# Making the rotary tables earlier and packing attention weights on another engine, in a two-layer encoder kernel

## The chip, the core and the metric

The kernel runs on one core of a Trainium2 chip. A core has five engines that run their own instruction streams in order and wait for one another through semaphores: PE (TensorE, matrix multiply), DVE (VectorE), ACT (ScalarE), POOL (GpSimd) and SP, which here only issues transfers from device memory. The metric is device time in microseconds (us); the lower the better. What one queue issues in a row is carried by 16 transfer engines.

## What is computed

Two layers of a streaming encoder over 256 positions of width 1024. The change lies in the first mixer, multi-head latent attention. Cut to that:

```python
mod = silu(c) @ ada_w[i] + ada_b[i]
sh1, sc1, g1, sh2, sc2, g2 = jnp.split(mod, 6, axis=-1)
h = modulate(rmsnorm(x, norm_g[i, 0]), sh1, sc1)        # h * (1 + sc1) + sh1
proj = h @ w_in                                         # 1024 -> 384 + 256 + 32
c_q  = rmsnorm(proj[..., :384], q_norm)
c_kv = rmsnorm(proj[..., 384:640], kv_norm)
ang = positions[..., None] * inv_freq                   # rotary tables
cos, sin = jnp.cos(ang), jnp.sin(ang)
k_rope = apply_rope(proj[..., 640:], cos, sin)
q  = (c_q @ w_uq).reshape(..., 16, 64 + 32)             # per head: 64 plain, 32 rotary columns
kv = (c_kv @ w_ukv).reshape(..., 16, 64 + 64)           # per head: 64 of the key, 64 of the value
q_rope = apply_rope(q[..., 64:], cos, sin)
o = softmax over the chunk-causal mask of (q_nope k_nope + q_rope k_rope) * scale, times v
x = x + g1 * (o @ w_out)
```

A dense feed-forward layer, a Mamba-2 mixer and a mixture of eight experts follow; the change does not touch them.

## The kernel before

Everything is 128 partitions wide. Activations are held transposed (`xT`, `h32`: 8 chunks of 128 features by 256 positions). Weights come in 1 MB pieces into eight buffers called `raw`; a new piece can only be issued once the instructions that read an old one have let its buffer go. The order in which instructions stand on each engine is not the order of the program text: a scheduler of the framework sets it when the kernel is built, from its own estimate of when each thing is ready, and from then on each engine runs its list strictly in order.

The start, in the order of the text: SP issues the first half of the constants (`cst`), x, small vectors (`vecs`), the modulation weights of units 0 and 2, two pieces of `w_in`, units 1 and 3, the last piece of `w_in`, the positions (`pos_i`, 128 KB, L407) and the rest of the constants. ACT squares x and takes a root (L413, L415), DVE makes the reciprocal `r` of it (L416), PE transposes x (L421) and spreads `r` over the partitions (L317). The modulation rows of a unit are eight matmuls (L247), a copy by DVE (`row`, L250) and four tiny matmuls (L258); then come the gains (L261, L269), the modulated activations (`tt` L330 on DVE, `h` L332 on ACT) and the projection with `w_in` (L438), first with chunks 0 to 3, and after units 1 and 3 with chunks 4 to 7.

The rotary tables (`ct`, `st`, L447 to L466) are made after that: DVE turns the positions into angles and brings them into range with eleven short instructions of 256 columns, each of which needs the one before it, and ACT takes two sines, ahead of which it loads the table of that function. They are first read by the rotation of the key (L499, L500).

GpSimd fills the mask rows of `qT` and `kT` (L471 to L478) with eight memsets that it begins at once, and copies the rotated key to the other heads (L521).

[...] A block of heads (L596) is its queries, two pairs of heads of attention (scores L570 and L571, maxima L573 and L574, exponentials L577 and L579, scaling L582 and L583, transposes L586 and their copy `pT` L588, values L591 to L593, `aT` L159), and a modulation unit whose sum DVE makes in seven long steps (`acc`, L220, 512 columns each).

Of the kernel before, what the change touches and what calls it, by code (L numbers as in the profile page):

```python
# [20 lines left out]
P = 128  # L21
S = 256
# [47 lines left out]
def rows(ap, n, off=0):  # L70

    return bass.AP(tensor=ap.tensor, offset=ap.offset + off, ap=[[P, n], [1, P]])


def bcast(ap, n, off=0, parts=P):

    return bass.AP(tensor=ap.tensor, offset=ap.offset + off, ap=[[0, parts], [1, n]])
# [3 lines left out]
def body(ctx: ExitStack, tc, x, c, positions, ada_w, ada_b, norm_g,  # L81
# [69 lines left out]
    def packed(src):  # L151

        k, h, n = src.shape[1:]
        t = hlp.tile([P, 1024], F32, tag="whi", name="wcp")[:, :k * h * n]
        A.copy(t.rearrange("p (k h n) -> p k h n", k=k, h=h), src)
        return t.rearrange("p (k m) -> p k m", k=k)

    def split(hi, lo, src):
# [94 lines left out]
    def ada_columns(units, rows):  # L253

        ps = pt("m")
        for i, (u, row) in enumerate(zip(units, rows)):
            for m in range(4):
                PE.matmul(ps[:, 4 * i + m:4 * i + m + 1], row[:, m * P:(m + 1) * P], one4, start=i == m == 0,  # L258
                          stop=True, skip_group_check=True)
        for i, u in enumerate(units):  # L260
            V.tensor_add(mod[:, 0, 4 * u:4 * u + 4], ps[:, 4 * i:4 * i + 4], vecT[:, 0, 4 * u:4 * u + 4])  # L261
# [3 lines left out]
    def make_gsc(i, t, k0=0, k1=DC):  # L265

        sc = mod[:, i, 24 * t + 8 + k0:24 * t + 8 + k1]
        g = vecT[:, 0, 96 + 16 * i + 8 * t + k0:96 + 16 * i + 8 * t + k1]
        V.scalar_tensor_tensor(gsc[:, i, t, k0:k1], sc, 1.0, g, op0=ALU.add, op1=ALU.mult)  # L269
# [108 lines left out]
    with ExitStack() as lctx:  # L378
# [11 lines left out]
        SP.dma_start(cst[:, 0:C_V], consts[:, 0:C_V])  # L390
        x_in = load(x[0], 2)
        V.reduce_sum(one4, ident.rearrange("p (g q) -> p g q", g=4)[:, :, 0], axis=AX.X)
        SP.dma_start(vecs[0:96, 0, :], rows(ada_b, 96))
        SP.dma_start(vecs[96:128, 0, :], rows(norm_g, 32))
        aw = {0: ada_load(0, 0)}
# [7 lines left out]
        u3 = ada_w[0, :, 1536:2048]  # L403
        aw[3] = [load(u3[0:512, :], 4), load(u3[512:768, :], 2), load(u3[768:1024, :], 2)]
        win += [win_load(6, 2)]
        pos_i = mi.tile([P, S], I32, tag="t2", name="pos_i", bufs=2)
        SP.dma_start(pos_i, bcast(positions, S))  # L407
        SP.dma_start(cst[:, C_V:], consts[:, C_V:C_KEY])


# [6 lines left out]
        for q in range(4):  # L417
            ps = pt("mm")
            for i in range(4):
# [2 lines left out]
            A.copy(xT[:, 2 * q:2 * q + 2, :], ps.rearrange("p (a s) -> p a s", a=2))  # L422
        r = spread(pt("n"), r)
        vec_block(0, 128)
        ada_columns((0, 2), [ada_rows(aw[u]) for u in (0, 2)])
        make_gsc(0, 0, 0, 4)
        normmod(0, 0, r, range(4), whole=h32)

        ps_kv, ps_rq, ps_q = pt("mm"), pt("mm"), pt("mm")

        kv = [(ps_kv[:, t * S:(t + 1) * S], t == 0, slice(QL + t * P, QL + (t + 1) * P)) for t in range(2)]
        rq = [(ps_rq[:, 0:S], True, slice(2 * P, 3 * P)),
              (ps_rq[:ROPE, S:2 * S], False, slice(QL + KVL, QL + KVL + ROPE))]
        qq = [(ps_q[:, t * S:(t + 1) * S], t == 0, slice(t * P, (t + 1) * P)) for t in range(2)]

        def win_mm(k, regions):
            for ps, first, sl in regions:
                PE.matmul(ps, win[k // 3][:, k % 3, sl], h32[:, k, :], start=first and k == 0, stop=k == DC - 1,  # L438
                          skip_group_check=True)
        for k in range(4):  # L440
            win_mm(k, kv + rq + qq)
        ada_columns((1, 3), [ada_rows(aw[u]) for u in (1, 3)])
        make_gsc(0, 0, 4, 8)
        normmod(0, 0, r, range(4, 8), whole=h32)


        ct = mp.tile([P, S], F32, name="ct")  # L447
        st = mp.tile([P, S], F32, name="st")
# [15 lines left out]
        A.activation(st, ang, AF.Sin)  # L464
        V.scalar_tensor_tensor(kk, ang, -1.0, ang, op0=ALU.mult, op1=ALU.max)
        A.activation(ct, kk, AF.Sin, bias=halfpi, scale=-1.0)  # L466


        qT = mp.tile([98, NH, S], F32, name="qT")
# [1132 lines left out]
```

## Time and profile before

| | us |
|---|---|
| median of 3 runs | 1297.62 |
| lowest and highest of them | 1292.73, 1299.51 |
| the profiled execution | 1294.19 |
| its span, from first to last instruction | 1292.4 |
| PE busy in the span | 1243.5 |
| DVE, ACT, POOL busy | 841.1, 695.4, 16.9 |

The rows of the profile are times in one execution. "Busy" of PE is modelled and includes waits of a started matmul, so what bounds a stretch is better read from the chain of waits, which goes back from the last instruction to what released it. A timeline row gives the start, the length, the engine, the source line, the operation, what it writes and reads, and how many instructions are merged; in brackets is how long the engine had been idle and what ended it. An fp32 matmul is recorded as two instructions.

### The profile page before, as it was taken

How to read it: one execution, taken by the hardware profiler on the slowest of the kernel's cores; microseconds unless marked ns; L12 is line 12 of the kernel's file. 1: busy time of each engine (PE TensorE's matmuls, PEld its weight loads, DVE VectorE, ACT ScalarE, POOL GpSimd, SP SyncE). 2: the span in 40 equal slices, each digit the busy share in tenths (PEclk: the TensorE clock that was granted, in tenths of full speed). 3: DMA queues.
4: the chain of work that ended last, by engine and by line, in shares of the span. 5: the costliest groups of instructions: out<-in, count | busy, mean ns of one | idle time of the engine just before them, and what ended most of it. 6: DMA issues, size and time to landing. Idle time of an engine off the chain costs nothing.

```text
span 1292.4 us, 21070 instructions
## 1 busy us (share of the span) xinstructions
PE 1243.5 (96%) x8200; PEld 997.4 (77%) x8200; DVE 841.1 (65%) x1293; ACT 695.4 (54%) x1158; POOL 16.9 (1%) x16
## 2 busy tenths in 40 slices
PE   6999999999999999998999999999999999999996
PEld 4677899999988999996648875488855788888652
DVE  3387787787779788853048870388902789988412
ACT  2468554455567767524157650477603676777302
POOL 4000000000000000000000000000000000000000
PEclk9899989999989999997999999999999999999998
DMA  9786569887933466425999999999999999998895
GB/s 341 284 299 216 196 226 361 317 303 268 339 116 131 148 207 233 164 98 196 422 421 420 420 395 413 420 421 420 384 388 421 421 420 383 391 346 315 327 421 214
DMA packets 104747, 407.96 MB, mean 316 GB/s; under 512 B 10418, under 2 KB 16063, under 8 KB 70975
## 3 DMA queue, kind: packets, MB, share of 16 engines
q1 hardware_dynamic: 104638, 406.53, 81.5%
q8 instruction: 66, 1.08, 0.3%
q14 instruction: 43, 0.34, 0.1%
HBM read 405.46 MB, written 1.05 MB: 315 GB/s over the span
## 4 chain that ended last, share of the span: by engine, by line
PE 88%; DMA 4%; ACT 3%; DVE 3%; issue 1%; SPq 0%; DVEq 0%; ACTq 0%
PE a L1280 18%; PE a L1372 11%; PE y L1325 10%; PE y L1391 4%; PE y L347 3%; PE y L349 3%; PE y L348 3%; PE gu L347 3%; PE gu L349 3%; PE gu L348 3%; PE in L349 2%; PE in L347 2%; PE in L348 2%; DMA raw<-in_moe_w_down_dram 2%; PE mm L438 2%; PE mm L505 2%
## 5 line engine op out<-in xcount | busy, mean ns | idle before, releaser
L159 DVE TENSOR_TENSOR wlo<-raw,whi 128x1024 fp32r<-128x1024 f32 x395 | 466.5, 1219 | 85.9 <-ACT whi L159 84.4
L159 ACT CAST whi<-raw 128x1024 fp32r<-128x1024 f32 x395 | 403.9, 1051 | 188.5 <-PE a L1280 42.5
L1372 PE MATMUL a<-raw,xe 128*64 128x384 f32 (+3 forms) x1280 | 161.5, 412 | 0.0
L1280 PE MATMUL a<-wlo,xe_hi 128*128 128x512 f32 (+1 forms) x464 | 153.6, 344 | 0.3
L1280 PE MATMUL a<-whi,xe_lo 128*128 128x512 f32 (+1 forms) x464 | 152.5, 341 | 0.0
L1372 PEld LDWEIGHTS a<-raw,xe 128*64 128x64 f32 x1280 | 91.8, 135 | 68.1 <-issue 50.9
L1293 DVE TENSOR_TENSOR sg<-sg,a 128x512 f32<-128x512 f32 (+2 forms) x36 | 22.0, 641 | 156.8 <-PE a L1372 144.9
L1280 PE MATMUL a<-whi,xe_hi 128*128 128x256 f32 (+1 forms) x464 | 111.6, 345 | 7.7 <-ACT whi L159 7.7
L220 DVE SCALAR_TENSOR_TENSOR acc<-raw,cond,acc 128x512 f32<-128x512 f32 x140 | 104.3, 757 | 2.8 <-ACT acc L218 1.2
L347 PE MATMUL gu<-hT_hi,whi 128*128 128x256 f32 x352 | 99.9, 284 | 1.2 <-ACT hT_hi L334 1.2
L1280 PEld LDWEIGHTS a<-wlo,xe_hi 128*128 128x128 f32 x464 | 87.5, 189 | 16.4 <-DVE wlo L159 3.6
L348 PE MATMUL gu<-hT_lo,whi 128*128 128x256 f32 x352 | 99.7, 283 | 0.0
L349 PE MATMUL gu<-hT_hi,wlo 128*128 128x256 f32 x352 | 99.4, 282 | 0.0
L1280 PEld LDWEIGHTS a<-whi,xe_lo 128*128 128x128 f32 x464 | 87.6, 189 | 9.8
L1280 PEld LDWEIGHTS a<-whi,xe_hi 128*128 128x128 f32 x464 | 76.1, 188 | 23.9 <-ACT whi L159 14.9
L1391 PE MATMUL y<-raw,at 128*64 128x512 f32 (+1 forms) x364 | 81.4, 586 | 0.9 <-DMA raw<-in_moe_w_down_dram 0.7
L347 PE MATMUL in<-hT_hi,whi 128*128 128x256 f32 (+1 forms) x264 | 76.0, 288 | 0.7 <-DVE r L303 0.7
L349 PE MATMUL in<-hT_hi,wlo 128*128 128x256 f32 (+1 forms) x264 | 75.5, 287 | 0.5 <-DVE wlo L159 0.5
L348 PE MATMUL in<-hT_lo,whi 128*128 128x256 f32 (+1 forms) x264 | 74.7, 283 | 0.0
L347 PEld LDWEIGHTS gu<-hT_hi,whi 128*128 128x128 f32 x352 | 67.3, 191 | 1.4 <-ACT hT_hi L334 1.4
L349 PEld LDWEIGHTS gu<-hT_hi,wlo 128*128 128x128 f32 x352 | 67.4, 192 | 0.0
L348 PEld LDWEIGHTS gu<-hT_lo,whi 128*128 128x128 f32 x352 | 67.3, 191 | 0.0
(398 smaller groups left out, 2245.4 us busy)
## 6 DMA issues: line engine op xcount, KB each, us to landing
raw<-in_moe_w_gate_dram SPq DMA_DIRECT2D x88, 1024.0 KB, 6.7
raw<-in_moe_w_up_dram SPq DMA_DIRECT2D x88, 1024.0 KB, 12.2
raw<-in_moe_w_down_dram SPq DMA_DIRECT2D x85, 1024.0 KB, 15.6
raw<-in_ada_w_dram SPq DMA_DIRECT2D x46, 1024.0 KB, 7.1
raw<-in_ssm_w_in_dram SPq DMA_DIRECT2D x20, 1024.0 KB, 5.3
raw<-in_ffn_w_down_dram SPq DMA_DIRECT2D x11, 1024.0 KB, 8.6
raw<-in_ffn_w_gate_dram SPq DMA_DIRECT2D x10, 1024.0 KB, 8.2
raw<-in_ffn_w_up_dram SPq DMA_DIRECT2D x10, 1024.0 KB, 8.9
```

Source lines behind the costliest of these rows:

```text
L159: return A.copy(hi, src), V.tensor_sub(lo, src, hi)
L220: V.scalar_tensor_tensor(acc, w[k // 4][:, k % 4, :], cond[:, k:k + 1], acc, op0=ALU.mult, op1=ALU.add)
L347: PE.matmul(ps, whi, ahi, start=(first and i == 0), stop=False, skip_group_check=skip)
L348: PE.matmul(ps, whi, alo, start=False, stop=False, skip_group_check=skip)
L349: PE.matmul(ps, wlo, ahi, start=False, stop=(last and i == n - 1), skip_group_check=skip)
L438: PE.matmul(ps, win[k // 3][:, k % 3, sl], h32[:, k, :], start=first and k == 0, stop=k == DC - 1, skip_group_check=True)
L505: PE.matmul(ps, lhs(k), rhs(k), start=(k == 0), stop=(k == n - 1))
L1280: PE.matmul(bank[:, o:o + n], a[:, j, :], w[:, m], start=f, stop=l, skip_group_check=True)
L1293: V.tensor_mul(self.sg[:, sl], self.sg[:, sl], self.acc["u", b][:, :n])
L1325: PE.matmul(self.y[b], a, w[:, b * 512:(b + 1) * 512], start=f, stop=l, skip_group_check=True)
L1372: PE.matmul(bank[FEW * h:FEW * (h + 1), o // 2:(o + n) // 2], self.xhi[:, j, :], w[:, h, :], start=first, stop=last, skip_group_check=True)
L1391: res = PE.matmul(self.y[c0 // 512][FEW * h:FEW * (h + 1), c0 % 512:c0 % 512 + n], self.at[t][:, FEW * h:FEW * (h + 1)], ws[h], start=t == ...
```

## The change

Three edits. The load of the positions is issued right after that of x, ahead of the small vectors and all modulation weights. The block that makes `ct` and `st` is moved, unchanged, ahead of the first modulation columns. And the copies of `packed` are written for GpSimd in place of ACT. Lines from L390 on move with it: the angle block is now L424 to L445, the projection L460.

```diff
@@ packed
         t = hlp.tile([P, 1024], F32, tag="whi", name="wcp")[:, :k * h * n]
-        A.copy(t.rearrange("p (k h n) -> p k h n", k=k, h=h), src)
+        G.tensor_copy(t.rearrange("p (k h n) -> p k h n", k=k, h=h), src)
@@ loads
         x_in = load(x[0], 2)
         V.reduce_sum(one4, ident.rearrange("p (g q) -> p g q", g=4)[:, :, 0], axis=AX.X)
+        pos_i = mi.tile([P, S], I32, tag="t2", name="pos_i", bufs=2)
+        SP.dma_start(pos_i, bcast(positions, S))
         SP.dma_start(vecs[0:96, 0, :], rows(ada_b, 96))
...
         win += [win_load(6, 2)]
-        pos_i = mi.tile([P, S], I32, tag="t2", name="pos_i", bufs=2)
-        SP.dma_start(pos_i, bcast(positions, S))
         SP.dma_start(cst[:, C_V:], consts[:, C_V:C_KEY])
@@ tables: this block now stands behind vec_block(0, 128), ahead of ada_columns((0, 2), ...)
         ct = mp.tile([P, S], F32, name="ct")
         st = mp.tile([P, S], F32, name="st")
         ang = mi.tile([P, S], F32, tag="t1", name="ang", bufs=2)
         kk = mi.tile([P, S], F32, tag="tr", name="kk", bufs=2)
         V.tensor_copy(ang, pos_i)
         V.tensor_scalar(ang, ang, cst[:, C_FREQ:C_FREQ + 1], None, op0=ALU.mult)
         V.tensor_scalar(kk, ang, 1.0 / (2 * math.pi), None, op0=ALU.mult)
         V.tensor_scalar(kk, kk, MAGIC, None, op0=ALU.add)
         V.tensor_scalar(kk, kk, MAGIC, None, op0=ALU.subtract)
...
         for v in pieces:
             V.scalar_tensor_tensor(ang, kk, -v, ang, op0=ALU.mult, op1=ALU.add)
         V.tensor_scalar(ang, ang, 3.1415925, -3.1415925, op0=ALU.min, op1=ALU.max)
         A.activation(st, ang, AF.Sin)
         V.scalar_tensor_tensor(kk, ang, -1.0, ang, op0=ALU.mult, op1=ALU.max)
         A.activation(ct, kk, AF.Sin, bias=halfpi, scale=-1.0)
```

Since a scheduler sets the order, what the edits move is read from the built programs. On DVE, at the start of the program (`one4` is L392, the casts L710 belong to a later layer and were put there as filling), the lines with a plus are new at this place:

```order
 L392 TENSOR_REDUCE few<-cst 128x1
 L710 CAST ej<-cst 128x128 x2
+L430 CAST ang<-pos_i 128x256
+L431 TENSOR_SCALAR ang<-ang,cst 128x256
+L432 TENSOR_SCALAR kk<-ang 128x256
+L433 TENSOR_SCALAR kk<-kk 128x256
+L434 TENSOR_SCALAR kk<-kk 128x256
+L441 SCALAR_TENSOR_TENSOR ang<-kk,ang 128x256 x4
+L442 TENSOR_SCALAR ang<-ang 128x256
+L444 SCALAR_TENSOR_TENSOR kk<-ang 128x256
 L416 RECIPROCAL r<-r 128x2
 L211 COPY vecT<-n 128x128
```

The whole block of angles, eleven instructions, now stands ahead of the reciprocal `r`, which every modulated activation needs; before, it stood among and behind the last `tt` of the second half.

On PE, in the same place (transposes of x, spreading of `r`, and the first two units' modulation rows):

```order
 L421 MATMUL mm<-cst,raw 128x128 x16
-L247 MATMUL mm<-raw,cond 32x512
 L317 MATMUL n<-cst,r 128x128 x2
 L210 MATMUL n<-cst,vecs 128x128
-L247 MATMUL mm<-raw,cond 32x512 x7
+L247 MATMUL mm<-raw,cond 32x512 x8
 L258 MATMUL m<-few,row 128x1 x4
 L247 MATMUL mm<-raw,cond 32x512 x8
```

Before, one of the eight row matmuls of unit 0 stood ahead of the spreading of `r`; now all eight stand behind it.

On ACT, in the attention, around the rotary queries of the second block of heads (`t_662`), before:

```order
L556 ACTIVATE qT<-mm 64x256 x2
L155 COPY wcp<-raw 128x384
L562 ACTIVATE qT<-t_662 32x256 x3
L588 COPY pT<-tp 128x384 x2
L562 ACTIVATE qT<-t_662 32x256
L556 ACTIVATE qT<-mm 64x256 x2
```

and the same place now:

```order
L556 ACTIVATE qT<-mm 64x256
L159 CAST aT_hi<-o 128x256
L556 ACTIVATE qT<-mm 64x256
L562 ACTIVATE qT<-t_662 32x256
L588 COPY pT<-tp 128x384
L562 ACTIVATE qT<-t_662 32x256 x3
L556 ACTIVATE qT<-mm 64x256 x2
L588 COPY pT<-tp 128x384
```

The copy of 384 columns is gone from ACT, and the two `pT`, which stood together, now stand apart, one ahead of three rotary query copies and one behind two plain ones. GpSimd gets ten copies: four (the key's two and the first block's two) ahead of its four copies L521, and six behind them.

## Rows read from the trace of the kernel before

**Rows 1.** The page, chain of waits: shares of the span by engine
```profile
PE 88%; DMA 4%; ACT 3%; DVE 3%; issue 1%; SPq 0%; DVEq 0%; ACTq 0%
```
**Rows 2.** Windows: busy us (x instructions) of PE, PEld, DVE, ACT, POOL; granted clock, DMA, GB/s
```profile
44.00:63.00 19.00, 18.35 (x78) 13.39 (x79) 7.57 (x23) 12.09 (x25) 0.24 (x1) 0.84 0.60 207
80.00:100.00 20.00, 17.84 (x110) 14.56 (x108) 15.38 (x42) 16.98 (x47) 0.00 (x0) 1.00 0.86 307
```
**Rows 3.** Chain of waits at the start: start us, us, engine, tile, line
```profile
11.48 1.43 PE mm L247 x2
12.92 0.64 PE n L317 x4
13.67 1.88 PE mm L247 x14
...
17.37 2.38 PE mm L247 x16
...
23.15 13.25 PE mm L438 x48
```
**Rows 4.** Timeline: the weight load of unit 2's fifth row matmul
```profile
18.67 0.14 PEld L247 LDWEIGHTS mm<-raw,cond 128*32 128x32 f32 x4 [0.37 <-DMA raw<-in_ada_w_dram]
```
**Rows 5.** Timeline of the start, POOL and DVE; the last row for comparison
```profile
0.76 3.51 POOL L471 MEMSET qT<- 2x4096 f32 x1 [0.29 <-POOLq L1590]
...
1.05 3.29 DVE L712 CAST uones<-ones 128x128 fp32r<-128x128 f32 x1
...
4.66 3.57 DVE L710 CAST ej<-cst 128x128 fp32r<-128x128 f32 x2
...
8.02 1.10 POOL L472 MEMSET qT<- 2x1024 f32 x1
...
12.02 0.17 DVE L416 RECIPROCAL r<-r 128x2 f32<-128x2 f32 x1 [3.79 <-ACT r L415]
...
12.62 0.95 POOL L477 MEMSET kT<- 1x1024 f32 x1
...
45.69 0.22 DVE L711 CAST uones<-cst 128x128 fp32r<-128x128 f32 x1
```
**Rows 6.** Timeline: four of the DVE rows that make the angles
```profile
44.37 0.28 DVE L451 CAST ang<-pos_i 128x256 f32<-128x256 int32 x1
...
45.83 0.29 DVE L453 TENSOR_SCALAR kk<-ang 128x256 f32<-128x256 f32 x1
...
46.81 1.80 DVE L462 SCALAR_TENSOR_TENSOR ang<-kk,ang 128x256 f32<-128x256 f32 x4
...
48.97 0.43 DVE L465 SCALAR_TENSOR_TENSOR kk<-ang 128x256 f32<-128x256 f32 x1
```
**Rows 7.** Chain of waits from the second projection half to the queries
```profile
44.65 10.74 PE mm L438 x36
...
64.18 16.36 PE mm L505 x60
```
**Rows 8.** The packing copies: count, ns min/median/max, first and last start, forms
```profile
L155 ACT COPY wcp<-raw x10: 500/816/1047, 51.5 to 96.4; 128x768 f32<-128x768 f32 x4, 128x384 f32<-128x384 f32 x4, 128x1024 f32<-128x1024 f32 x2
```
**Rows 9.** Groups of instructions by shape, POOL: busy us, mean ns, idle before
```profile
L521 POOL COPY kT<-kT 32x1024 f32<-32x1024 f32 x1 | 1.0, 1034 | 0.1
```
**Rows 10.** Timeline: POOL's last copy of the key, and a sum on DVE
```profile
64.97 1.89 POOL L521 COPY kT<-kT 32x2048 f32<-32x2048 f32 x1
...
65.39 2.01 DVE L220 SCALAR_TENSOR_TENSOR acc<-raw,cond,acc 128x512 f32<-128x512 f32 x1
```
**Rows 11.** That sum's line from 60 to 140 us: ns min/median/max, first and last start
```profile
L220 DVE SCALAR_TENSOR_TENSOR acc<-raw,cond,acc x39: 731/747/2010, 65.4 to 137.6; 128x512 f32<-128x512 f32 x39
```
**Rows 12.** Chain of waits in the attention: two ACT steps of it
```profile
96.46 0.40 ACT wcp L155
...
98.19 0.49 ACT pT L588
```
**Rows 13.** SP's own waits from 60 to 120 us: total, times, longest
```profile
SPq L127 <- ACT wcp L155: 14.2, 3, 10.3
```

More of the change, by code (lines that the diff above doesn't have):

```diff
@@ L424, in body @@
         vec_block(0, 128)
[L425 to L444, printed above, removed]
         ct = mp.tile([P, S], F32, name="ct")
@@ L466, in body, with win_mm @@
         A.activation(ct, kk, AF.Sin, bias=halfpi, scale=-1.0)
+        ada_columns((0, 2), [ada_rows(aw[u]) for u in (0, 2)])
+        make_gsc(0, 0, 0, 4)
+        normmod(0, 0, r, range(4), whole=h32)
+        ps_kv, ps_rq, ps_q = pt("mm"), pt("mm"), pt("mm")
+        kv = [(ps_kv[:, t * S:(t + 1) * S], t == 0, slice(QL + t * P, QL + (t + 1) * P)) for t in range(2)]
+        rq = [(ps_rq[:, 0:S], True, slice(2 * P, 3 * P)),
+              (ps_rq[:ROPE, S:2 * S], False, slice(QL + KVL, QL + KVL + ROPE))]
+        qq = [(ps_q[:, t * S:(t + 1) * S], t == 0, slice(t * P, (t + 1) * P)) for t in range(2)]
+        def win_mm(k, regions):
+            for ps, first, sl in regions:
+                PE.matmul(ps, win[k // 3][:, k % 3, sl], h32[:, k, :], start=first and k == 0, stop=k == DC - 1,
+                          skip_group_check=True)
+        for k in range(4):
+            win_mm(k, kv + rq + qq)
+        ada_columns((1, 3), [ada_rows(aw[u]) for u in (1, 3)])
+        make_gsc(0, 0, 4, 8)
+        normmod(0, 0, r, range(4, 8), whole=h32)
         qT = mp.tile([98, NH, S], F32, name="qT")
```

## The prediction, made before the changed kernel had run

> **What bounds the kernel now.** I read the chain of waits of the whole span first: 88% of it is PE, and no other engine has more than 4% [rows 1]. So a change elsewhere counts only where PE stands waiting, and the question is where that is in the stretch that the change touches, the first 140 us or so. Behind that stretch the instructions stand in the same order before and after (but for a few loads by SP), so what the first 140 us gain or lose is handed on as it is.
>
> From 0 to 23 us the chain goes back and forth. PE transposes x, runs one row matmul of unit 0 until 12.92, spreads `r`, and runs the other seven until 15.55; then come a DVE copy, tiny matmuls and the eight of unit 2 [rows 3]. The fifth of these waits 0.37 us for its load [rows 4]: here transfers set the end. From 23.15 us on the projection runs on PE without a gap [rows 3].
>
> From 44.65 to 80.5 us the chain is PE alone: 10.74 us of projection in one piece, and later 16.36 us of the key, value and query matmuls in one piece [rows 7]. PE is busy 18.35 of 19.00 us between 44 and 63 [rows 2]. ACT works 12.09 us there and DVE 7.57, beside PE.
>
> From 80 us on it changes. Between 80 and 100 us ACT is busy 16.98 of 20.00 us, DVE 15.38 and PE 17.84 [rows 2], and the chain steps from PE to ACT and back. Two of its ACT pieces show what the change can reach: 0.40 us of `wcp` at 96.46, and the `pT` at 98.19 that PE waits for [rows 12].
>
> **The tables leave ACT and DVE at 44 to 55 us: worth nothing.** Two sines and eleven DVE instructions go from a stretch in which PE is the chain [rows 7]. What hides them is the projection, and its matmuls are the same in number. If that cover were gone, 18.35 of 19.00 us leaves 0.65 us at most [rows 2]. I take 0.
>
> **The load of the positions, 128 KB, is put ahead of about 4 MB of modulation weights.** All pieces behind it come later by its bytes. The windows give 207 to 307 GB/s as means [rows 2], which makes 0.43 to 0.63 us; the first unit pays nothing, since it doesn't wait for a load, and unit 2 pays all of it, as it already waits [rows 4]. Taken alone: +0.4. It is not added to the next term: whoever is late by more than that finds the weights there.
>
> **The block of angles ahead of the reciprocal: +2.9.** Undisturbed, the block takes 0.28 for the cast, about 0.33 for each of five scalings (three of them fill 45.83 to 46.81), 1.80 for the four reductions and 0.43 for the last one [rows 6]: 4.2 us. It can start behind the casts L710, at 8.23 [rows 5], if the positions are there; x, issued just ahead of them, is even transposed by 11.48 [rows 3]. So it would end at 12.4 and the reciprocal at 12.6 instead of 12.19 [rows 5]. PE only gets to the spreading of `r` at 12.92 [rows 3], so this costs nothing.
>
> But it is not undisturbed. GpSimd's memsets run from 0.76 to 13.57, six of them from 8.02 on, 0.92 us apart [rows 5]. A cast on DVE that takes 0.22 us when GpSimd is idle took 3.29 beside the memset of 3.51 us, and ended as that one ended, at 4.3; the two casts at 4.66 waited in the same way, until 8.23, and the memset behind them was stretched to 1.10 [rows 5]. So this kind of DVE instruction and a memset don't run side by side. The casts that waited were ready and went two at a time; those of the block depend on one another, so that after each GpSimd, whose memsets depend on nothing, can put one in. I expect turn by turn: the cast squeezes in at 8.3 (or waits for one memset more), and each of the four scalings behind it waits for a memset, with 0.8 us lost on each over its 0.33. That is 3.2 us: the block ends near 15.7, `r` near 15.9, and `r` is spread from 16.1 instead of 12.92. The four reductions I count as free of this, as no row shows one of their kind held by a memset.
>
> On PE the pause is 3.2 us long, and nothing can fill it, since the one row matmul that stood ahead of it stands behind it now. The group of eight takes 2.0 us (2.38 less the wait of 0.37) against 1.88 for seven [rows 3, 4]: +0.1. The wait of 0.37 for the load disappears, as everything behind is later. Sum: 3.2 + 0.1 - 0.4 = +2.9 us at 23.15, and from there PE has no gap to take it back.
>
> Bounds: from below +0.4 (nothing is held; the load alone). From above, all memsets go first, to 13.57, and then the whole block of 4.2 and the reciprocal of 0.17 [rows 5, 6]: `r` at 17.9, 5.1 late, so 5.1 + 0.1 - 0.4 = +4.8. Nearest to what the casts did is taking turns, which lies between, and I take +2.9. The granted clock is 0.84 as a mean from 44 to 63 us [rows 2], so PE is at times at the lower of its two levels; if the longer pause put the 16 row matmuls there, they would take up to 4 us more. I don't count on that, but it widens the upper end.
>
> [...]
>
> **The packing copies leave ACT: -1.2.** Ten copies go, 7.1 us by their median lengths [rows 8]. Six of them, the key's two and the first two blocks' four, lie before 80.5 us, where PE is the chain: 0. The four between 80 and 97 us take 2 x 0.82 + 2 x 0.50 = 2.6 us of ACT's 16.98 [rows 2, 8]. On the chain lie 0.40 us of them [rows 12]. The rest shifts ACT forward; the `pT` at 98.19 stands ahead of three rotary copies now, but the second one stands behind two more. I take 0.4 for the step itself and 0.8 for the rest of the attention, in which ACT and DVE take turns with PE in a new order. Bounds: -2.6 and one more us for the order, -3.6; on the other side, an in-order engine that gets a worse list, +1.5.
>
> **The same copies on GpSimd: 0, with a tail.** POOL copies 1024 columns in 1.03 us [rows 9], as fast as ACT, though these copies have gaps in their reads, which no row shows; at twice the time they'd still be early. The first four are made as soon as their weights land, some 15 us before PE reads them, while DVE has little to do. The others wait only for their buffers. Loads behind a `wcp` waited up to 10.3 us for ACT to get to it [rows 13], and will be issued sooner; but transfers stand nowhere in the chain between 44 and 140 us, so that buys nothing. The price is on DVE: a sum L220 that takes 0.75 us took 2.01 beside a GpSimd copy [rows 10, 11]. Six copies are still to come then, about 1.2 us to a block of heads [rows 8, 9], so 3.5 us of DVE in all. Between 80 and 100 us DVE is idle 4.6 us [rows 2], and the block copied near 70 us meets a DVE that nobody waits for at once. I take 0; the bound is +3.5.
>
> **Sum.** +2.9 - 1.2 = +1.7 us. On the profiled execution, 1294.19, that is 1295.9; on the median, 1297.62, it is 1299.3. The four times of before differ by 6.8 us, so I put the time between these two, at 1298, and measure the rivals from 1296.3, which is 1.7 less.
>
> **The rivals.** First: nothing is held at the start (the memset lets a short instruction pass), and ACT's relief is worth its bound: +0.4 - 3.6 = -3.2, so 1293. For it speaks that ACT is the busiest beside PE from 80 to 100 us [rows 2]; against it the cast of 3.29 us [rows 5]. Second, on the other side: GpSimd in DVE's way, at both places. All memsets go first (+4.8), and in the attention DVE binds and pays the 3.5 us of copies, less the 0.4 that leaves the chain: +7.9, so 1304. It decides once DVE's gaps in the attention don't lie where the copies come; 15.38 of 20.00 us is not far from full [rows 2], and L220 has been caught once [rows 10]. Third: the change hides itself. The tables were hidden by PE, the load costs 0.4, copies change nothing: 1296.7.
>
> **How the numbers follow.** Forecast 0.45, first rival 0.2, second 0.2, third 0.15. About half a percent, 6.5 us, is what a measurement of this kernel can tell from no change; from 1297.62 this is below 1291.1 and above 1304.1. The first rival passes that line only with a low run, the second half of the time: faster 0.08, same 0.81, slower 0.11. The range reaches from 1292 to 1304: the first rival's 1293 and the second's 1304 at its ends, with a little for the runs' own spread on the lower side; outside lie the upper half of the second rival and the low tail of the first.
>
> **What would show it.** In the trace of after: the block of angles on DVE lasts 7 to 8 us instead of 4.2, its scalings alternate with memsets, `r` is there near 16 us, PE pauses from 11.5 to about 16, and the first projection matmul starts near 26.0 instead of 23.15. If it starts by 23.6, the first rival or the third is right. From there the starts of the second half (44.65) and the key matmuls (64.18) are late by the same amount; a change of that amount between 44 and 80 us would prove me wrong on PE's chain. The first feed-forward matmul, or the last value product of the attention, is late by less than the projection was, by 1.2 us; if by more, GpSimd's copies are in DVE's way, and L220 shows rows of over 1 us around 70 and 88 us.

## The result, and the profile after

The changed kernel takes 1302.46 us as a median of 7 runs (1301.24 to 1305.05); the kernel before, on the same chip, 1297.16 (1292.73 to 1300.12). The medians lie 5.3 us apart. The ratio is 1.0052 (6.8 us), with a 95% interval of 1.0033 to 1.0070: slower, by 4.3 to 9.1 us. One execution of the twelve of "changed, fills everywhere" below took 2046.17 us at a mean granted clock of 0.554, and its ratio leaves it out.

| us | before | after |
|---|---|---|
| the profiled execution | 1294.19 | 1302.46 |
| its span | 1292.4 | 1300.6 |
| mean granted clock of PE in the span | 0.978 | 0.973 |
| PE busy | 1243.5 | 1245.8 |
| DVE, ACT, POOL busy | 841.1, 695.4, 16.9 | 845.8, 689.8, 26.5 |

The profiled execution of the kernel before lies 3.0 below its median, that of the changed kernel on it. So the two profiles stand 8.2 us apart, 2.9 more than the medians.

The chain of waits of after, from the start to the second half of the projection (start us, us, engine, tile, line; the projection is L460 now). It answers to [rows 3, 7]:

```profile
2.36 6.38 DMA pos_i<-in_positions_dram
...
16.19 1.23 PE n L317 x4
17.62 3.62 PE mm L247 x16
...
22.01 1.86 PE m L258 x8
23.88 3.64 PE mm L247 x16
...
28.28 1.88 PE m L258 x8
...
31.73 13.73 PE mm L460 x48
```

The spreading of `r` (L317) starts 3.27 us later than in [rows 3]. The first projection starts 8.58 later, at 31.73 instead of 23.15. So there are two losses: a pause of PE, and 5.3 us more (8.58 less 3.27) in the work behind it. The rows give the second: both groups of row matmuls take 3.62 and 3.64 where they took about 2.0, the groups of tiny ones 1.86 and 1.88 where they took 1.05 and 1.06, L317 1.23 for 0.64. All of it runs at about half speed.

What DVE and GpSimd do in the same time (timeline: start, length, engine, line, operation), to be read beside [rows 5, 6]:

```profile
8.76 0.51 DVE L430 CAST ang<-pos_i 128x256 f32<-128x256 int32 x1 [0.53 <-DMA pos_i<-in_positions_dram]
9.07 1.09 POOL L474 MEMSET qT<- 1x1024 f32 x1
9.31 1.00 DVE L431 TENSOR_SCALAR ang<-ang,cst 128x256 f32<-128x256 f32 x1
...
12.43 1.00 DVE L434 TENSOR_SCALAR kk<-kk 128x256 f32<-128x256 f32 x1
13.22 1.10 POOL L477 MEMSET kT<- 1x1024 f32 x1
13.47 1.80 DVE L441 SCALAR_TENSOR_TENSOR ang<-kk,ang 128x256 f32<-128x256 f32 x4
15.30 0.29 DVE L442 TENSOR_SCALAR ang<-ang 128x256 f32<-128x256 f32 x1
...
15.98 0.16 DVE L416 RECIPROCAL r<-r 128x2 f32<-128x2 f32 x1
```

Four scalings take 1.00 us each while memsets run. The fifth, L442, takes 0.29, since the last memset is over. The four reductions take 0.45 each as always, though a memset of 1.10 lies beside the first two.

The windows show the granted clock (third number from the end: what PE got, as a share of its full clock). First after, then the kernel before:

```profile
9.00:60.00 51.00, 40.68 (x178) 24.37 (x177) 14.35 (x33) 10.22 (x19) 8.68 (x10) 0.73 0.88 323
12.00:15.00 3.00, 0.00 (x0) 0.00 (x0) 2.83 (x6) 2.59 (x4) 2.32 (x3) 1.00 1.05 385
15.00:18.00 3.00, 1.81 (x9) 1.24 (x13) 1.35 (x5) 0.92 (x2) 0.00 (x0) 0.53 1.05 388
30.00:33.00 3.00, 1.65 (x5) 1.34 (x6) 2.24 (x8) 1.68 (x4) 0.00 (x0) 0.50 1.05 387
```
```profile
9.00:60.00 51.00, 45.51 (x222) 28.24 (x220) 11.81 (x35) 15.92 (x30) 4.57 (x6) 0.90 0.88 322
24.00:27.00 3.00, 3.00 (x9) 1.64 (x9) 0.01 (x1) 0.55 (x2) 0.00 (x0) 0.66 1.05 388
45.00:48.00 3.00, 3.00 (x8) 2.34 (x8) 2.83 (x10) 0.91 (x2) 0.00 (x0) 0.50 1.04 384
```

In after PE stands still from its last transpose, at 11.4, to 16.19, which is 4.8 us. From 15 us on the clock is at 0.50, and stays there until nearly 36; in single microseconds from 9 to 60 us both kernels show 1.00, 0.50 and, where it changes, a value between. The kernel before keeps 1.00 up to 21 us, but it isn't free of this either: its clock falls at 21 to 27 and at 42 to 51, each time within or right behind a stretch in which PE waits for the modulation.

From 71 to 87 us, while key, value and queries are made, the chain goes through DVE, where [rows 7] had 16.36 us of PE in one piece (chain of after, and PE's waits between 60 and 100 us):

```profile
74.92 1.30 DVE acc L220
76.25 2.27 DVE acc L220
...
79.33 1.20 DVE acc L220
...
86.94 4.12 PE mm L505 x18
```
```profile
PE mm L505 <- DVE v_sb L537: 0.8, 1, 0.8
```

The three sums lie beside GpSimd's copies: L521 from 73.00 to 77.97, `wcp` from 78.93 to 80.89. Undisturbed each takes 0.75 [rows 11]; together they lose 2.5 us. The kernel before lost 1.3 of this already, on its one sum beside L521 [rows 10]. The copies of the value, `v_sb`, stand behind them on DVE, as they did before; PE waits 0.84 us for the third of them.

Just ahead of the first score the clock falls once more. The last ten query records there (timeline, after and then before) and the granted clock around them (window of after):

```profile
93.53 4.01 PE L505 MATMUL mm<-lat,wcp 128*128 128x256 f32 x10
83.01 2.32 PE L505 MATMUL mm<-lat,wcp 128*128 128x256 f32 x10
```
```profile
93.00:96.00 3.00, 3.00 (x11) 2.42 (x11) 2.40 (x6) 0.00 (x0) 0.00 (x0) 0.62 1.08 393
```

In single microseconds the clock is 0.50 at 94 to 97, while before it is 1.00 from 78 to 92. Of the fourteen kernels here and below, six of the seven with packing on GpSimd have such a dip at 83 to 97 us, and none of the seven with packing on ACT has one there. Why, no run shows.

How late the same matmul starts, against the kernel before (each from the profiled execution; the runs with names are told below):

| matmul, start before | after | packing alone | tables alone | fill ahead of r | fills in before | fills in after |
|---|---|---|---|---|---|---|
| spreading of `r`, 12.85 | +3.3 | +0.4 | +3.3 | +3.3 | 0.0 | +3.3 |
| first projection, 23.15 | +8.6 | +0.2 | +5.2 | +2.0 | +0.2 | +2.0 |
| first key matmul, 62.2 | +9.4 | +0.6 | +5.8 | +2.2 | -3.8 | -1.8 |
| first score, 85.5 | +11.9 | +1.9 | +5.8 | +4.7 | -3.8 | +0.4 |
| first feed-forward matmul, 163.3 | +13.9 | +3.2 | +6.5 | +5.7 | -2.6 | +1.8 |
| first of the Mamba layer, 365.9 | +11.9 | -0.2 | +6.3 | +4.7 | -2.6 | +1.3 |
| first expert matmul, 591.8 | +9.9 | -2.4 | +6.2 | +2.6 | +0.3 | +2.2 |
| span | +8.2 | -4.2 | +4.9 | +5.2 | 0.0 | +2.1 |

Up to the first key matmul the change costs 9.4, from there to the feed-forward layer 4.5 more, and 5.7 come back until the end. The executions are not equally typical: packing alone (1290.02 us, its median 1296.54) was profiled in the fastest of its twelve executions, the fills in before (1294.26, 1291.80) in one of the slower. So the last rows of a column are not yet the time of its kernel.

### The profile page after: what moved, and what is told of

It is laid out like the page before. It is cut to its first block, busy times and chain, and to the rows that moved or that the text cites. A ratio compares the mean times of both kernels' runs of the same rounds, so it can differ in the third digit from the quotient of the medians.

```text
span 1300.6 us, 21067 instructions
## 1 busy us (share of the span) xinstructions
PE 1245.8 (96%) x8200; PEld 997.3 (77%) x8200; DVE 845.8 (65%) x1293; ACT 689.8 (53%) x1148; POOL 26.5 (2%) x26
## 3 DMA queue, kind: packets, MB, share of 16 engines
HBM read 405.46 MB, written 1.05 MB: 313 GB/s over the span
## 4 chain that ended last, share of the span: by engine, by line
PE 85%; DMA 4%; DVE 4%; ACT 4%; issue 2%; SPq 0%; DVEq 0%; ACTq 0%
PE a L1280 18%; PE a L1372 12%; PE y L1325 9%; DMA raw<-in_moe_w_down_dram 4%; PE y L347 3%; PE y L1391 3%; PE gu L347 3%; PE y L349 3%; PE gu L349 3%; PE y L348 3%; PE gu L348 3%; PE mm L460 2%; PE in L349 2%; PE in L347 2%; PE in L348 2%; PE a L1189 2%
## 5 line engine op out<-in xcount | busy, mean ns | idle before, releaser
L220 DVE SCALAR_TENSOR_TENSOR acc<-raw,cond,acc 128x512 f32<-128x512 f32 x140 | 106.0, 769 | 3.3 <-ACT acc L218 1.7
```

The source lines that it names most:

```text
L220: V.scalar_tensor_tensor(acc, w[k // 4][:, k % 4, :], cond[:, k:k + 1], acc, op0=ALU.mult, op1=ALU.add)
```

## The experiments

All but the changed kernel itself were timed in twelve executions beside 35 of the kernel before (medians 1295.92 to 1296.60). A difference of 0.001 in a ratio is 1.3 us.

| run | ratio to before | 95% interval |
|---|---|---|
| changed kernel | 1.0052 | 1.0033 to 1.0070 |
| packing alone | 1.0000 | 0.9986 to 1.0014 |
| tables alone | 1.0033 | 1.0015 to 1.0052 |
| changed, small memsets late | 1.0035 | 1.0018 to 1.0052 |
| changed, fill ahead of `r` | 1.0014 | 0.9996 to 1.0032 |
| changed, angles behind the reciprocal | 1.0046 | 1.0028 to 1.0065 |
| the same, packing on ACT | 1.0006 | 0.9990 to 1.0021 |
| before, `r` late | 1.0035 | 1.0020 to 1.0051 |
| before, fills | 0.9958 | 0.9939 to 0.9977 |
| before, fills, packing on GpSimd | 0.9967 | 0.9954 to 0.9981 |
| changed, fills everywhere | 0.9981 | 0.9970 to 0.9992 |
| the same, packing on ACT | 0.9980 | 0.9962 to 0.9997 |
| before, fills, angles meant for 24 us | 1.0003 | 0.9986 to 1.0020 |

### The two halves of the change apart

Packing alone: the kernel before with one line of the change, by which GpSimd makes the ten copies of key and query weights into `wcp` [rows 8].

```diff
-        A.copy(t.rearrange("p (k h n) -> p k h n", k=k, h=h), src)
+        G.tensor_copy(t.rearrange("p (k h n) -> p k h n", k=k, h=h), src)
```


> Only the packing copies go from ACT to GpSimd; positions, angle block and tables stay where they were before. Theory (the late reciprocal and the slow projections after it are the whole loss): the start is as before, r near 11.4 us and the first projection near 23.2; the second half's projection at 44.65 within 1 of before; the time lies between 1 below and 3 above the kernel before. Rival 'the packing is the loss': the queries' 18 matmuls and what follows come 3 us or more later than before and the time is about 5 above. Rival 'the packing is a gain that the tables hide': the time is 2 or more below.

1.0000. The start is as before (+0.2 at the first projection). From its key matmuls to the first score its delay grows by 1.3 us, and this is the clock, not a wait for DVE: here too a sum beside a copy takes up to 2.26 us, but PE doesn't wait for `v_sb`, and the ten query records ahead of the first score take 3.73 us for 2.32, at a granted clock of 0.50 from 85 to 88:

```profile
84.00:87.00 3.00, 3.00 (x11) 2.39 (x10) 2.83 (x5) 1.00 (x3) 0.00 (x0) 0.61 1.05 386
```

The time as a whole neither gains nor loses: the interval goes from 1.8 below to 1.8 above.

Tables alone: the changed kernel with that line undone.

> The positions come early and the angle block stands ahead of the reciprocal, as in the changed kernel; the packing copies stay on ACT. Theory: the whole loss of the start is here, r near 16 us, PE without work from about 11.5, a granted clock near 0.5 from 15 to 36 and the first projection near 31.7; the time is 4 to 8 above the kernel before, like the changed kernel's. Rival 'the packing is the loss': the first projection may be late, but the time at the end is within 1.5 of the kernel before.

1.0033, 4.3 us above. So the loss lies with the tables. The first projection came at 28.38, not near the 31.7 expected, and the granted clock did not stay near 0.5 until 36 (chain, then one window):

```profile
17.62 3.62 PE mm L247 x16
...
22.00 1.05 PE m L258 x8
23.06 1.92 PE mm L247 x16
...
28.38 13.48 PE mm L460 x48
```
```profile
21.00:24.00 3.00, 2.19 (x24) 1.38 (x24) 0.69 (x1) 0.00 (x0) 0.00 (x0) 0.84 1.03 389
```

Up to 22 us PE runs the same instructions at the same times as in the changed kernel. There the clock stays at 0.50 until nearly 36 us; here it is back to full by 22, and the tiny matmuls take 1.05 instead of 1.86. So behind the same instructions the lower clock lasted 7 us in one execution and 20 in the other.

### Is it the pause or what stands in it?

Small memsets late: the changed kernel with six memsets held back until `ct` is there.

```diff
+        gate = mp.tile([P, 1], F32, name="gate")
+        with tc.issue_after(G.tensor_copy(gate, ct[:, 0:1]).ins):
             G.memset(qT[96:98, :, 128:192], 1.0)
...
             G.memset(kT[96:97, :, 64:128], NEG)
```


> The changed kernel with its six small memsets of qT and kT held back until the cosine table is there, so that nothing on GpSimd runs beside the angle block; every other order is the changed kernel's. Theory: the four scalings take about 0.3 us each instead of 1.0, the reciprocal ends near 13.2 instead of 16.1, PE's pause shrinks by 2.9, and if the lower clock comes from that pause most of it goes too: first projection at 24 to 26 (31.7 in the changed kernel, 23.15 before), time 4 to 7 below the changed kernel. If the lower clock comes whatever the pause, the first projection moves by 2.9 alone, to 28.8. Rival 'the order of the loads is the loss': the scalings are short and the end is as late as in the changed kernel.

```profile
13.27 1.22 PE n L317 x4
14.70 2.96 PE mm L247 x16
...
24.80 14.56 PE mm L460 x48
```

The start did as the theory said: with the memsets away a scaling takes 0.31 to 0.36, `r` is spread at 13.27, PE's pause is 2.1 us, and the first projection comes at 24.80, though L317 (1.22) and the first row matmuls (2.96) still run slow. The time didn't: 1.0035, 2.2 us below the changed kernel where 4 to 7 were expected. The profile has it at +1.7 at the first projection, +5.3 at the feed-forward layer, +1.4 at 437 us and +7.1 at the end. One of these steps can be read. It lies at 450 to 457 us, where nothing was edited (a window of this run, then of the kernel before):

```profile
453.00:456.00 3.00, 3.00 (x15) 2.97 (x15) 0.40 (x3) 2.42 (x6) 0.00 (x0) 0.50 0.72 283
```
```profile
453.00:456.00 3.00, 3.00 (x25) 2.73 (x24) 3.00 (x7) 2.08 (x5) 0.00 (x0) 1.00 0.47 104
```

A dip of the clock costs 3 us there in this execution. Two others have one as deep at 446 to 459 (the packing-on-ACT run with angles behind the reciprocal, the fills in before); the kernel before has none. So the profiles differ by such dips too, and a single one doesn't give the time of its kernel to better than some 3 us.

Fill ahead of `r`: the changed kernel, with 20 matmuls that nothing reads between the last transpose and the spreading of `r`.

```diff
-        r = spread(pt("n"), r)
+        fill = pt("m")
+        for _ in range(20):
+            with tc.issue_after(tail.ins):
+                tail = PE.matmul(fill[:, 0:P], ident, ident, start=True, stop=True)
+        with tc.issue_after(tail.ins):
+            r = spread(pt("n"), r)
```


> The changed kernel with 20 idle 128x128 matmuls of the identity on PE between the last transpose and the spreading of r (extra work that nothing reads), so that PE doesn't stand still while the angle block holds the reciprocal. Theory that the lower clock follows from PE standing still: the granted clock stays at or near 1.0 from 15 to 30, eight row matmuls take about 2 us instead of 3.6, the first projection starts near 26 (16.19 + the 10 us that lie between spread and projection in the kernel before), time 4 to 6 below the changed kernel. Rival 'the row matmuls of 32 columns bring the lower clock themselves': the clock falls to about 0.5 soon after 16 all the same and the first projection stays near 31.7.

```profile
16.19 0.71 PE n L317 x4
17.01 2.71 PE mm L247 x24
...
25.19 13.29 PE mm L465 x48
```

`r` is as late as in the changed kernel, 16.19. But L317 takes 0.71 instead of 1.23, 24 records of row matmuls (twelve matmuls) take 2.71, where 16 took 3.62, the granted clock is 1.00 from 9 to 24 us (then 0.62 at 24 to 27, where the kernel before has 0.66), and the first projection comes at 25.19 instead of 31.73. Time: 1.0014, 4.9 us less than the changed kernel, known to about 3.3. Work that does nothing makes the kernel faster: that here it is PE's standing still, and not the row matmuls themselves, that brings the lower clock is shown by this pair.

### Late by other means

Angles behind the reciprocal: the changed kernel with the block queued on DVE behind `r`; and the same with the packing on ACT.

```diff
-        V.reciprocal(r, r)
+        recip = V.reciprocal(r, r)
...
+        with tc.issue_after(recip.ins):
-        V.tensor_copy(ang, pos_i)
+            V.tensor_copy(ang, pos_i)
```


> The changed kernel with the angle block queued behind the reciprocal on DVE; all else in its order, the packing copies on GpSimd too. Theory (the whole loss is that the block stands ahead of the reciprocal): r near 11.4 to 12.9 us, first projection within 0.7 of 23.2, time within 2 of the kernel before, some 5 to 7 below the changed kernel, and the same as with the packing alone. Rival 'the early load of the positions is the loss': it stays 4 or more above the kernel before.

> As the run before, but with the packing copies on ACT: early positions and early tables alone, with nothing ahead of the reciprocal. Theory: first projection within 0.7 of 23.2, time within 2 of the kernel before; the difference to the run before says once more what the packing on GpSimd costs by itself, expected between 2 below and 2 above. Rival 'early tables help once they hold nothing': 1 to 2 below the kernel before, since 4.2 us of DVE and 0.8 of ACT leave 44 to 49.

The first missed (1.0046); its time is that of the rival, the early load. The second held by its time (1.0006) but not by its start (first projection at 26.23, 3.1 late). As it loads the positions early too, the load is not the loss. That the packing parts the two by 5.2 us was not expected, and their profiles don't show it (spans of 1297.1 and 1298.7): this stays open. The chain of the first says why its start is late:

```profile
17.55 0.61 DVE row L250
18.20 1.86 PE m L258 x8
20.07 3.64 PE mm L247 x16
```

`r` is in time, but now the block stands ahead of the copy `row` (L250), which came at 15.57 before and comes at 17.55. PE waits for that instead, from about 15.6 (it is busy 0.59 us of the three from 15) to 18.20, and the clock falls all the same (0.50 at 18 to 24). I had looked only at what stands behind the block first. From 11.5 to 20 us DVE has a short step that PE waits for every 4 us, and no gap between two of them holds 4.2 us and turns with GpSimd.

`r` late: the kernel before with 17 multiply-adds of a tile that nothing reads ahead of the reciprocal.

```diff
+        dmy = mh.tile([P, S], F32, name="dmy")
+        held = V.scalar_tensor_tensor(dmy, x_in[:, 0, 0:S], 0.25, x_in[:, 0, 0:S], op0=ALU.mult, op1=ALU.add)
+        for _ in range(16):
+            with tc.issue_after(held.ins):
+                held = V.scalar_tensor_tensor(dmy, dmy, -0.25, dmy, op0=ALU.mult, op1=ALU.add)
+        with tc.issue_after(held.ins):
+            V.reciprocal(r, r)
```


> The kernel before with 17 multiply-adds on a tile of their own (extra work that nothing reads) ahead of the reciprocal on DVE, about 7.8 us, and no other difference but that five row matmuls stand ahead of the spreading of r. Theory: r near 16, the spreading 3 to 3.5 late, PE idle for 2 to 4 us before it, the granted clock at 0.5 for some microseconds after it, first projection 5 to 9 late, time 4 to 7 above the kernel before. Rival 'a late reciprocal costs its own pause and no more': first projection 3 to 3.5 late and the granted clock at 1.0 until 21; time about 3 above.

```profile
16.05 0.71 PE n L317 x4
16.87 1.02 PE mm L247 x6
...
25.03 13.48 PE mm L444 x48
```

The time is as expected, 1.0035, the profile is nearer to the rival's: no lower clock before 24 us, first projection 1.9 late, span +3.3. Here five row matmuls stood ahead of L317, so PE worked until 14.2, but for 0.4 us, and then stood still for only 1.9 us. In this execution a late `r` costs its pause and no more. With the small memsets late, L317 and the row matmuls did run slow behind a pause of 2.1 us, hardly a longer one; what parts the two is not shown. And this execution is the fastest of its twelve (1297.51 us, the median 1301.54), with a mean granted clock of 0.979 where the other eleven have 0.972 to 0.977. So it may lack a dip that the others have, and it doesn't decide between theory and rival.

### Taking the clock out of both kernels

Fills in before: the kernel before with 3 matmuls that nothing reads while DVE copies the second row, and 6 while modulation and normalisation are made, in both halves.

```diff
+    def fill(ps, n, after):
+        for _ in range(n):
+            with tc.issue_after(after.ins):
+                after = PE.matmul(ps[:, 0:P], ident, ident, start=True, stop=True, skip_group_check=True)
+        return after
@@ ada_columns
         ps = pt("m")
+        (free, _), (_, last) = tail[-2:]
+        held = fill(free, 3, last)
         for i, (u, row) in enumerate(zip(units, rows)):
-            for m in range(4):
-                PE.matmul(ps[:, 4 * i + m:4 * i + m + 1], row[:, m * P:(m + 1) * P], one4, start=i == m == 0,
-                          stop=True, skip_group_check=True)
+            with tc.issue_after(held.ins) if i else ExitStack():
+                for m in range(4):
+                    last = PE.matmul(ps[:, 4 * i + m:4 * i + m + 1], row[:, m * P:(m + 1) * P], one4,
+                                     start=i == m == 0, stop=True, skip_group_check=True)
+        fill(free, 6, last)
```


> The kernel before with idle 128x128 matmuls of the identity (extra work that nothing reads) in the two pauses of PE ahead of each half of the latent projection: 3 while DVE copies the second row, 6 while modulation and normalisation are made (19.8 to 23.2 and 41.0 to 44.7 in the kernel before). Theory that PE's pauses bring the lower clock: the granted clock doesn't fall to 0.66 at 24 to 27 nor to 0.50 and 0.68 at 45 to 51, the first 48 projections take about 11 us instead of 13.25, the time is 2 to 5 below the kernel before. Rival: the clock falls as before whatever fills the pauses, and the time is the same, or 0.3 above by the fillers.

```profile
23.38 11.85 PE mm L451 x48
...
43.49 8.15 PE mm L451 x36
```
```profile
24.00:27.00 3.00, 3.00 (x14) 2.03 (x13) 0.38 (x1) 0.91 (x2) 0.00 (x0) 1.00 1.05 385
45.00:48.00 3.00, 3.00 (x16) 2.64 (x15) 2.76 (x8) 0.75 (x2) 0.00 (x0) 1.00 1.06 388
```

0.9958: 5.4 us faster than the kernel before by the ratio, 4.8 by the medians (1291.80 against 1296.58). The granted clock is 1.00 from 9 to 60 us. The first half of the projection takes 11.85 instead of 13.25 [rows 3], the same 36 records of the second half 8.15 instead of 10.74 [rows 7], together 4.0 us; at the first key matmul the profile is 3.8 ahead. By 592 us this lead is gone in the profiled execution, which has two dips of the clock that the kernel before hasn't (0.50 at 136 to 139 and 447 to 453); it is one of the slower of its twelve. By the timed runs the fills beat both kernels.

The same with the packing on GpSimd:

> The kernel before with the idle matmuls in the pauses of PE ahead of both halves (extra work that nothing reads) and with the packing copies on GpSimd; the tables stay where they were. It gives the packing a start that the clock doesn't disturb. Theory (packing on GpSimd is worth nothing or costs, by DVE's sums beside the copies and by the order): between the same time as with the idle matmuls alone (4.8 below the kernel before) and 3 above that. Rival 'packing off ACT is worth its 1.2 us or more': 1 to 3 below the idle matmuls alone.

0.9967 (1291.25 against 1295.92): as fast, or 1.2 us slower. No gain from the packing here either.

The changed kernel with all fills, and the same with the packing on ACT:

> The changed kernel with idle matmuls (extra work that nothing reads) in all the pauses of PE: 20 ahead of the spreading of r, 3 and 6 ahead of each half of the projection. Theory (its loss is about 3 us of pause behind the angle block, the rest the clock, and the packing): granted clock 1.0 from 9 to 54, first projection near 26, the first 48 projections in about 11.8 us; time 4 to 9 below the changed kernel, and still 3 to 5 above the kernel before with the same idle matmuls, that is, 1 to 2 below the kernel before or equal to it. Rival 'the clock is all of it': equal to the kernel before with the idle matmuls, 4.8 below the kernel before.

> As the run before, with the packing copies on ACT. Theory: first projection near 26 as there; the end 0 to 3 earlier than there, since DVE's sums near 74 to 80 us don't lie beside GpSimd's copies. Rival 'packing on GpSimd helps': 1 or more later than there.

0.9981 and 0.9980. With the clock held at 1.00 from 9 to 54 us the changed kernel gains 9.2 us on itself (1.0052 to 0.9981) and the kernel before 5.4. So 3.8 us of the change's 6.8 go with the clock of this stretch; the other 3.0 remain, and are its pause and its packing (first projection +1.8 against the fills in before, first key matmul +1.9, first score +4.2, behind a clock of 0.50 at 83 to 86 that the fills in before don't have). The 3.8 come from four kernels and are known only to about 3.7 us, the 3.0 to about 2.8; firmer is the 9.2, known to about 2.8. The packing shows no difference in this pair.

Last, a try to put the block where DVE is idle, at 24 to 29 us:

```diff
+        done = normmod(0, 0, r, range(4), whole=h32)
+        with tc.issue_after(done.ins):
+            V.tensor_copy(ang, pos_i)
```


> The kernel before with the idle matmuls (extra work that nothing reads), the positions loaded early as in the changed kernel, and the angle block behind the first half's normalisation, near 24 to 29 us, where DVE and ACT do nothing (0.0 to 0.6 us of 3 in the windows from 27 to 36); packing on ACT. Theory (the tables leaving 44 to 55 us is worth nothing, the early load costs 0.4): within 1.5 of the kernel before with the idle matmuls, 3.3 to 5 below the kernel before. Rival 'tables made under cover do help, the changed kernel only put them at the wrong place': 1 to 4 below the idle matmuls alone.

```profile
12.43 1.02 DVE kk L450
...
16.19 1.22 PE n L330 x4
17.62 2.99 PE mm L255 x16
...
27.79 11.85 PE mm L472 x48
```

The edit missed its aim: `done` is an instruction of ACT, and it held back the two sines and not the DVE block, which still stands ahead of the reciprocal. So whether tables made at 24 us help was not tried. What this kernel shows instead is the block ahead of `r` with all fills but the 20 ahead of L317. It comes to 1.0003, against 0.9980 with them: those 20 matmuls are worth 3.0 us, known to about 3.2, and the row matmuls behind the pause take 2.99 where 1.9 is full speed.

## Why the prediction was right or wrong

The time, 1302.46, lies in the range of 1292 to 1304, 4.5 above the point, and on the side that was forecast. It lies below the 1304.1 from which the prediction would have called it slower. But the change was forecast at +1.7 and came at +5.3 by the medians, 6.8 by the ratio: the sum was three to four times too small, and the range held the time because the second rival reached that far. By its steps:

**The tables leaving 44 to 55 us: 0.** Not tried by itself. With the clock held, the tables alone are 2.0 us late at the first projection and 2.0 at the first key matmul (the last fills run with packing on ACT, less the fills in before), so nothing came back between the two, as forecast.

**The load early: +0.4.** Not tried by itself. With packing on ACT and the angles behind `r` the kernel that has it is 0.8 us slower than the kernel before (-1.3 to +2.7), so it costs little. That `pos_i` lands at 8.76, 0.53 later than DVE was ready, was not in the sum.

**The block ahead of the reciprocal: the mechanism held, the size didn't.** The turns with the memsets, the free reductions, `r` at 15.98 (forecast near 15.9) and L317 at 16.19 (16.1) came as worked out; holding the memsets back makes the scalings short (0.31 to 0.36 us). That the times fit so well has luck in it: a scaling lost 0.7 us and not 0.8, 2.7 in all for 3.2, and the 0.53 us for `pos_i` made up for it. And PE's pause is 4.8 us, where the prediction said 3.2: that is the delay of L317, and the 1.4 us that the one row matmul had filled are pause now too. In the trace the scalings are held by the memsets (1.00 for 0.29) and the reductions are not (0.45), while the sums L220, SCALAR_TENSOR_TENSOR like the reductions, are held beside GpSimd's copies (2.27 for 0.75). Why, no run shows.

The step that failed is the sentence behind the sum: "they would take up to 4 us more. I don't count on that". The clock did fall behind the pause. It took 5.3 us in the profile, net: 3.0 on the row matmuls (3.62 + 3.64 against 1.88 + 2.38 in [rows 3], the changes of +0.1 and -0.4 among it), 1.6 on the tiny matmuls and 0.7 on L317 and the one matmul behind it, groups that the bound left out. The first projection was 8.58 late, above the upper bound of 4.8 for this term. In the timed runs the clock of this stretch costs the changed kernel 3.8 us more than the kernel before, known to about 3.7 (both kernels with and without fills). The kernel before showed the sign: 0.84 as a mean from 44 to 63 us [rows 2], behind a wait of PE (1.6 us) that is shorter than the new one. The runs with this pause and with the 20 fills in it show what the standing still does to the clock here: 0.50 behind the pause, 1.00 with the fills. I had read the row of the 0.84 and priced it as a tail of the range; the half speed came in each of the three kernels that leave this pause unfilled (L317 at 1.22 or 1.23 in the changed kernel, the tables alone and the last run).

**Packing off ACT: -1.2.** No run shows the gain. Five pairs differ in the packing alone: 0.0, +1.2, +2.5, +5.2 and +0.1 us for GpSimd (packing alone, with fills, with the early tables, with angles behind `r`, with all fills). Four of them alone are within their uncertainty; their mean, 1.8, points to a cost rather than a gain. The ten copies are 7.4 us by the lengths in [rows 8], not the 7.1 of the prediction; nothing else was worked out from that.

**The same copies on GpSimd: 0, bound +3.5.** In the profile the price lies between. The signs that the prediction named came: L220 rows of 1.30, 2.27 and 1.20 us at 75 to 80 us, and a delay that grows from 9.4 at the first key matmul to 11.9 at the first score. But of these 2.5 us only about 1.0 is DVE's, with PE's wait of 0.84 for `v_sb`; the other 1.5 is the clock of 0.50 at 94 to 97, which the prediction didn't have. What was wrong is that "the block copied near 70 us meets a DVE that nobody waits for at once": nine sums stood ahead of `v_sb` in DVE's list where seven had stood, and PE waited.

**The delay handed on unchanged.** It held from the first projection to the key matmuls (8.6, 9.1, 9.4). Behind 140 us it did not: the delay was 13.9 at 163 us and fell to 9.9 by 592, in a stretch with the same order. Part of that looks like the clock again. Over the same work, from the first feed-forward to the first expert matmul, the mean granted clock is 0.97 in before and 0.98 in after; a hundredth of some 426 us is 4.3 us, and 4.0 came back. That the clock gave them back is argued from these rounded means, not shown by a run.

**The rivals.** The second, GpSimd in DVE's way, with 1304, has the right time by luck: the memsets did not all go first, the sums on DVE cost PE about 1.0 us and not 3.1, and what made up the rest was the clock, which no rival named.

## What to carry to other kernels

Before moving work ahead of something PE waits for, count what the pause does to the matmuls behind it: here a pause of 4.8 us, with `r` spread 3.3 us late, was followed by 5.3 more of half-speed work in the profile, and nine idle matmuls in each of two old pauses gained 5.4 us (3.0 to 7.9) without touching the algorithm. Work is free to move only into a gap that holds all of it between two steps that the busy engine waits for; being off the chain where it came from says nothing of the place where it goes. And copies on GpSimd weren't free beside DVE here (a sum of 0.75 us took up to 2.27): look at which of DVE's instructions they slow, and who stands behind. A stretch that got longer is not explained by a slow engine beside it until the wait for that engine, and the clock of the stretch, have been read.

## What the runs showed of the hardware

The lower clock's length differed between two executions behind the same instructions: 0.50 from 15 to nearly 36 us in the changed kernel, from 15 to 22 with the tables alone. Over the fourteen profiles the span mostly goes with the mean granted clock: 0.973 for 1300.6 and 1299.5 us, 0.978 for 1292.4 and 1297.6, 0.982 to 0.984 for 1288.2 to 1289.4. So do the timed runs of the kernel before, from 1291.67 us at 0.982 to 1303.47 at 0.971; those of the changed kernel don't (1302.46 at 0.973, 1303.73 at 0.982). Much of the spread of the kernel before looks like clock.

The granted clock in the windows is not always what the matmuls show. With the small memsets late (12 to 18 us) and in the last run (15 to 21) the column reads 1.00, while L317 takes 1.22 us instead of 0.64 and sixteen row matmul records 2.96 and 2.99 instead of about 1.9:

```profile
18.00:21.00 3.00, 2.56 (x16) 0.40 (x8) 0.36 (x1) 0.00 (x0) 0.00 (x0) 1.00 1.05 391
```

This is a window of the last run. Where the column and the durations differ, the durations decide what it cost.

In the changed kernel a DVE scaling of 128x256 took 1.00 us beside a memset of 1x1024 (L478) as beside one of 2x1024 (L476), 0.7 more than the 0.29 of L442 with no memset beside it; these memsets took 1.10 each, 0.95 in the kernel before.
